# Latent attention: heads made in groups of four, half of them inside the attention, with the modulation sums moved behind them

## The chip, the cores and the metric

The kernel runs on one core of a Trainium2 chip. The metric is the device time of one execution in microseconds (us). A matmul runs on PE and its weights are loaded by PEld; DVE, ACT and POOL are the vector, scalar and GpSimd engines; SP issues most of the DMAs. Every engine works through its own list of instructions in order, and waits there for what it needs from another engine.

## The reference

Two layers of an encoder over 1024 tokens of width 1024. The change lies in the first layer's mixer, a latent attention with 16 heads. Cut to that:

```python
proj = h @ w_in                                   # 1024 x (384 + 256 + 32)
q = (rms_norm(q_lat, g_qa) @ w_qb).reshape(B, S, 16, 96)
kv = (rms_norm(kv_lat, g_kva) @ w_kvb).reshape(B, S, 16, 64 + 64)
q = concat(q[..., :64], rope(q[..., 64:]))
k = concat(kv[..., :64], k_rope of all heads)
v = kv[..., 64:]
q, k = rms_norm(q, g_q), rms_norm(k, g_k)
o = softmax(q k^T * 96 ** -0.5) v                 # all 1024 keys for each of 1024 queries
return o.reshape(B, S, 1024) @ w_o
```

`rms_norm(x) = x * rsqrt(mean(x * x) + eps) * g`. Around the mixer stand a norm with a shift, scale and gate that come from a conditioning vector: `mod = silu(c) @ ada_w + ada_b`, six vectors of 1024 for each layer. An MLP follows, and then a second layer with a dilated attention and an MLP.

## The kernel before

Every large product is made from fp16 high and low parts in three matmuls: `mm3` multiplies high by high (L532), high by low (L533) and low by high (L534). The program in order of time: the norm, the input projection and the latents (`latT`, transposed, in fp16 parts); the **heads stage**, 119 to 265 us; the **attention**, to 613 us; then the output projection, the MLP and the second layer.

**The heads stage** (`mla`, the loop `for hf in range(2)`) has two passes over the 8 tiles of 128 tokens. Pass 0 makes heads 0 to 7, pass 1 heads 8 to 15. A tile is two groups of four heads: for each group PE makes the queries `pq` (9 matmuls of 384 columns) and the keys and values `pkv` (6 of 512 columns), each into one of the 8 PSUM banks. From the banks ACT squares them; DVE sums the squares (`hms`; L954 is a small TENSOR_SCALAR that adds the rope part of the key, `krss`); `rstd` (L126) turns sums into factors, with Ln and Exp on ACT (L132, L133) and three small DVE steps (L134 to L136); DVE scales the bank's contents into `st`; POOL turns the rope columns (`rope_q`, four operations, L635 to L638) and multiplies the rope part of the key by the factor (L973); ACT rounds `st` to fp16 (L981); POOL takes the low part from that (L982), and SP stores the tile `s` to a DRAM buffer `qkv`. A tile's banks come free when DVE has scaled them.

Inside pass 0 stand the last two quarters of the latents and the weights of pass 1 (`heads_load`, `heads_split`; L156 and L161 are the two steps of a split). Inside pass 1 stand the first loads of the attention, since heads 0 to 7 are whole by then: `fetch(h)` reads `q` and `k` of a head from `qkv` with transposing DMAs (L842), `ones(h)` loads a row of ones and the values, and `rowmax(0)` makes the 16 partial row maxima of head 0: one matmul of 512 columns into a bank `pmx` (L893) and one TENSOR_REDUCE on DVE (L895), each. `topmost`, `turn` and `mrow` turn the maxima into a row of `q`, which the scores of that head need.

**The attention** (L1181) is written out by hand as 128 slots, one for each of 16 heads and 8 tiles of 128 keys, and `pin_from` keeps every engine to the written order. In a slot n PE makes the scores (`scores`, 6 matmuls of 512 columns, L1207 to L1209, into two banks `pss`), two row maxima of a head to come, and the product with the values of slot n-3 (`av`, 24 small matmuls); POOL takes the low part of the weights of slot n-1 (L1226, `pp`); ACT makes the weights of slot n (`weights`: two Exp that read `pss`, L1218, and one rounding, L1219). DVE takes the maxima, and ends a head (`finish`). The PSUM banks are three of kind "s" (scores), three of kind "t" (row maxima and everything else) and two of kind "av". In every fourth slot `ada_step` adds one row block of the modulation matrices to a sum (`ada_sum`, L270 for the first, L271 for the others: DVE, 128x1024, from SBUF to SBUF); after eight of them PE and DVE finish the vector (`ada_end`).

Of the kernel before, what the change touches and what calls it, by code (L numbers as in the profile page):

```python
# [9 lines left out]
F32 = mybir.dt.float32  # L10
F32R = mybir.dt.float32r
F16 = mybir.dt.float16
# [3 lines left out]
ALU = mybir.AluOpType  # L16
# [25 lines left out]
class K:  # L42
# [83 lines left out]
    def rstd(self, ms, n, name, up=False, y=None):  # L126

        nc = self.nc
        y = self.sm(name + "y", n) if y is None else y
        l = self.sm(name + "l", n)  # L130
        t = self.sm(name + "t", n)
        nc.scalar.activation(l, ms, AF.Ln, bias=self.eps_y if up else self.eps)  # L132
        nc.scalar.activation(y, l, AF.Exp, scale=-0.5)  # L133
        nc.vector.scalar_tensor_tensor(t, ms, EPS * 2.0 ** 26 if up else EPS, y, op0=ALU.add, op1=ALU.mult)  # L134
        nc.vector.scalar_tensor_tensor(t, t, -0.5, y, op0=ALU.mult, op1=ALU.mult)
        nc.vector.scalar_tensor_tensor(y, t, 1.5, y, op0=ALU.add, op1=ALU.mult)  # L136
        return y
# [517 lines left out]
    def mla(self, xs, ada0, xs1, mods, tail):  # L655
# [5 lines left out]
        lt = lambda k, c, t: LT[t // 4][k][c // 2][:, c % 2, (t % 4) * P : (t % 4 + 1) * P]  # L661
        krw = self.M("krw", [P, 8, 32])
# [22 lines left out]
        with tc.tile_pool(name="psA", bufs=2, space=PSUM, reuse_waits="tile") as psp:  # L685
# [38 lines left out]
            def latents(tp, lats, m, pt):  # L724
# [7 lines left out]
                if tp % 2 == 0:  # L732
                    for k, x in enumerate(self.pair(self.G, "latT", (P, 2, 512))):
                        LT[half][k].append(x)
# [109 lines left out]
        def ones(h):  # L844

            hd = heads[h]
            nc.sync.dma_start(out=hd["kh"][QK : QK + 1, :], in_=self.onerow)
            v = hd["v"] = self.G("hv", (P, 8, 129), F16)
            nc.gpsimd.memset(v[:, :, 128:129], 1.0)
            nc.sync.dma_start(out=v[:, :, 0:128], in_=qkv[h][:, 384:512].rearrange("(t p) e -> p t e", p=P))  # L850
# [73 lines left out]
        with tc.tile_pool(name="psB", bufs=8, space=PSUM, reuse_waits="tile") as psp:  # L924
            B = lambda name: psp.tile([P, 512], F32, tag="b", name=self.nm(name))
            raw = None
            for hf in range(2):
                w = hw[hf]
                for t in range(NT):
# [12 lines left out]
                    st = [self.G("st", (P, 4, 192 if half else 256), F32) for b in range(2)]  # L942
                    s16 = [self.G("s16", (P, 4, 512), F16) for b in range(2)] if half else None
# [12 lines left out]
                    if half:  # L956
                        for b in range(2):
                            self.parts(s16[b][:, :, 448:512], s16[b][:, :, 384:448], kv4[b][:, :, 64:128], 2.0 ** -7)
                    i = (hf * NT + t) * 16
                    r = self.rstd(ms, 16, "hr", half, rall[:, i : i + 16] if half else None)  # L960
                    for b in range(2):
                        if not half:
                            nc.scalar.activation(st[b][:, :, 192:256], kv4[b][:, :, 64:128], AF.Copy)
# [3 lines left out]
                        if half:  # L967
                            nc.vector.scalar_tensor_tensor(st[b][:, :, 96:160], kv4[b][:, :, 0:64], 64.0,
                                                           rk.broadcast_to([P, 4, 64]), op0=ALU.mult, op1=ALU.mult)
                        else:  # L970
                            nc.vector.tensor_tensor(st[b][:, :, 96:160], kv4[b][:, :, 0:64],
                                                    rk.broadcast_to([P, 4, 64]), op=ALU.mult)
                        nc.gpsimd.tensor_tensor(st[b][:, :, 160:192], rk.broadcast_to([P, 4, 32]),  # L973
                                                kr[:, t : t + 1, :].broadcast_to([P, 4, 32]), op=ALU.mult)
                    for b in range(2):
                        h0 = hf * 8 + b * 4
                        if half:
                            self.rope_q(st[b][:, :, 64:96], t)
                            nc.vector.tensor_tensor(st[b][:, :, 0:64], st[b][:, :, 0:64],
                                                    gt[:, 0:64].unsqueeze(1).broadcast_to([P, 4, 64]), op=ALU.mult)  # L980
                            nc.scalar.activation(s16[b][:, :, 0:192], st[b], AF.Copy)  # L981
                            nc.gpsimd.tensor_tensor(s16[b][:, :, 192:384], st[b], s16[b][:, :, 0:192], op=ALU.subtract)  # L982
                            nc.sync.dma_start(out=qkv[h0 : h0 + 4, ts, :].rearrange("h t e -> t h e"), in_=s16[b])
                            continue
# [12 lines left out]
                    elif half:  # L997
                        for f, x in {0: ((fetch, 0),), 1: ((ones, 0), (fetch, 1)), 2: ((ones, 1),), 5: ((fetch, 2),),
                                     6: ((ones, 2),)}.get(t, ()):
                            f(x)  # L1000
                        for j in {3: (0, 1, 2), 4: (3, 4, 5), 5: (6, 7)}.get(t, ()):
                            [rowmax(0, j, b, B("pmx")) for b in range(2)]
                        if t == 5:
                            topmost(0)
                        elif t == 6:
                            turn(0, B("pmt"))
                            mrow(0)
# [14 lines left out]
        if half:  # L1022
            self.nseen += 1
            s_ = self.seen[:, self.nseen - 1 : self.nseen]
            for _ in range(2):
                nc.gpsimd.tensor_tensor(rall, rall, rall, op=ALU.mult)
            nc.vector.tensor_reduce(s_, rall, op=ALU.add, axis=AX.X)
# [1814 lines left out]
```

## Time and profile before

| | us |
|---|---|
| median of 3 runs | 3013.63 (3011.02 to 3015.2) |
| the profiled execution | 3010.92 |
| its span in the trace | 3009.1 |
| heads stage, first matmul of pass 0 to first score | 119.3 to 265.4 |
| attention, first score to the last product | 265.4 to about 613 |
| attention, 111 slots from 283 to 578 us | 2.66 each |

The profile gives busy time for each engine as a whole, for each stretch of time and for each group of like instructions ("line engine op out<-in xcount | busy, mean ns of one | idle time before, by what ended it"). An instruction's row in the timeline reads: start, duration, engine, line, operation, out<-in, and in brackets the idle time before it with what ended that. "PE pmx <- DVE mx" is a wait of PE for a bank `pmx` that DVE still read.

### The profile page before, as it was taken

The numbers are of one execution on the slowest core, as the hardware profiler recorded it, in microseconds if no ns is written. First come the engines' busy times: TensorE is split into PE (matmuls) and PEld (weight loads), VectorE is DVE, ScalarE is ACT, GpSimd is POOL, SyncE is SP. The second block draws the span as 40 slices with busy tenths as digits, with TensorE's granted clock in tenths as the row PEclk, the third lists the DMA queues.
The fourth block names the chain that finished last, engine by engine and source line by source line (L and its number), as shares of the span: only waits on it lengthen the run. The fifth ranks groups of instructions, "written<-read, shape, count | busy, mean of one in ns | idle before, by whom it ended". The sixth has DMA issues, their size and how long they took to land. (4 is left out here: it accounts for less than half of the span.)

```text
span 3009.1 us, 54541 instructions
## 1 busy us (share of the span) xinstructions
PE 2830.6 (94%) x20148; PEld 1678.5 (56%) x20148; DVE 2272.5 (76%) x4991; ACT 1660.7 (55%) x3411; POOL 938.6 (31%) x1372
## 2 busy tenths in 40 slices
PE   6877999999999999999999989998997989999998
PEld 5634566644444444443468878877885444444443
DVE  6687777648988876689758877776886789779565
ACT  4645888825455533542227877776664355555331
POOL 6688888800111000001123434353552002110010
PEclk9988999999999999999999999999999999999999
DMA  6264555424755689555536656665666556457663
GB/s 208 73 175 127 114 103 107 137 78 134 258 193 188 236 246 314 184 192 191 210 114 140 156 130 157 154 134 123 140 143 165 146 187 217 154 180 257 231 197 91
DMA packets 556656, 503.07 MB, mean 167 GB/s; under 512 B 275638, under 2 KB 448995, under 8 KB 556379
## 3 DMA queue, kind: packets, MB, share of 16 engines
q1 hardware_dynamic: 520698, 400.74, 47.4%
q0 software_dynamic: 25248, 87.22, 7.8%
q10 hardware_dynamic: 10432, 11.54, 1.5%
q8 instruction: 159, 2.61, 0.4%
q14 instruction: 119, 0.97, 0.1%
HBM read 317.40 MB, written 125.12 MB: 147 GB/s over the span
## 5 line engine op out<-in xcount | busy, mean ns | idle before, releaser
L532 PE MATMUL psm<-hf,wf 128*128 128x512 f16 x896 | 341.1, 381 | 5.0 <-ACT wf L156 5.0
L534 PE MATMUL psm<-hf,wf 128*128 128x512 f16 x896 | 335.7, 381 | 10.5 <-DVE wf L161 10.5
L533 PE MATMUL psm<-d,d 128*128 128x512 f16 x896 | 340.5, 380 | 4.7 <-DVE d L161 4.7
L533 PE MATMUL psm<-hf,wf 128*128 128x512 f16 x896 | 340.8, 380 | 0.0
L534 PE MATMUL psm<-d,d 128*128 128x512 f16 x896 | 340.4, 380 | 0.0
L532 PE MATMUL psm<-d,d 128*128 128x512 f16 x896 | 334.6, 379 | 0.3 <-ACT d L156 0.3
L1226 POOL TENSOR_TENSOR pp<-p,pp 128x1024 f16<-128x1024 f32 x125 | 275.4, 2209 | 56.3 <-ACT pp L1219 38.8
L532 PE MATMUL psproj<-wqk,hTp 128*128 128x256 f16 x1024 | 283.6, 277 | 0.0
L533 PE MATMUL psproj<-wqk,hTp 128*128 128x256 f16 x1024 | 282.9, 276 | 0.0
L534 PE MATMUL psproj<-wqk,hTp 128*128 128x256 f16 x1024 | 282.6, 276 | 0.0
L156 ACT ACTIVATE d<-ufr 128x1024 f16<-128x1024 f32 x112 | 117.8, 1052 | 207.9 <-PE psm L534 170.4
L895 DVE TENSOR_REDUCE mx<-pmx 128x1 f32<-128x512 f32 x256 | 172.9, 687 | 78.9 <-PE pmx L893 77.6
L161 DVE SCALAR_TENSOR_TENSOR d<-ufr,d 128x1024 f16<-128x1024 f32 x112 | 136.3, 1217 | 75.0 <-ACT d L156 74.9
L1218 ACT ACTIVATE p<-pss 128x512 f32<-128x512 f32 x256 | 149.9, 590 | 40.9 <-PE pss L1209 39.3
L2321 ACT ACTIVATE pd<-pd,dnb 128x192 f32<-128x192 f32 (+2 forms) x384 | 167.2, 436 | 4.3 <-POOL y L2250 2.2
L534 PEld LDWEIGHTS <-wf 128*128 128x128 f16 x896 | 87.8, 98 | 122.5 <-DVE wf L161 18.1
L532 PEld LDWEIGHTS <-wf 128*128 128x128 f16 x896 | 87.8, 98 | 113.2 <-ACT wf L156 10.8
L534 PEld LDWEIGHTS <-d 128*128 128x128 f16 x896 | 87.7, 98 | 110.5 <-issue 5.6
L271 DVE SCALAR_TENSOR_TENSOR adacc<-adaw,cond,adacc 128x1024 f32<-128x1024 f32 (+1 forms) x98 | 129.0, 1316 | 25.5 <-DMA adaw<-in_ada_w 24.6
L532 PEld LDWEIGHTS <-d 128*128 128x128 f16 x896 | 87.9, 98 | 106.3 <-issue 2.0
L533 PEld LDWEIGHTS <-d 128*128 128x128 f16 x896 | 87.7, 98 | 106.0 <-issue 1.6
L533 PEld LDWEIGHTS <-wf 128*128 128x128 f16 x896 | 87.9, 98 | 104.9 <-issue 1.8
(434 smaller groups left out, 8132.1 us busy)
## 6 DMA issues: line engine op xcount, KB each, us to landing
ufr<-uf SPq DMA_DIRECT2D x112, 512.0 KB
w2r<-in_mlp_w SPq DMA_DIRECT2D x96, 512.0 KB
adaw<-in_ada_w SPq DMA_DIRECT2D x80, 512.0 KB
w1r<-in_mlp_w SPq DMA_DIRECT2D x64, 512.0 KB
wqkr<-in_dil_w_in SPq DMA_DIRECT2D x96, 256.0 KB
wvr<-in_dil_w_in SPq DMA_DIRECT2D x34, 512.0 KB
qkv<-s SPq DMA_DIRECT2D x32, 512.0 KB
uf<-ub POOLq DMA_DIRECT2D x32, 512.0 KB, 3.8
```

The lines of the kernel that those rows point to most:

```text
L156: nc.scalar.activation(hi, src, AF.Copy, scale=scale)
L161: return nc.vector.scalar_tensor_tensor(lo, src, scale, hi, op0=ALU.mult, op1=ALU.subtract, accum_out=self.seen[:, self.nseen - 1 : self.n ...
L271: return self.nc.vector.scalar_tensor_tensor(acc, w, c, acc, op0=ALU.mult, op1=ALU.add)
L532: mm(out, lh, rh, start=first, stop=False)
L533: mm(out, lh, rl, start=False, stop=False)
L534: mm(out, ll, rh, start=False, stop=last)
L895: nc.vector.tensor_reduce(maxes[h][:, 2 * j + b : 2 * j + b + 1], ps, op=ALU.max, axis=AX.X)
L1218: nc.scalar.activation(p[:, b * 512 : (b + 1) * 512], ps[b], AF.Exp, scale=1.0 / self.ss)
L1226: eng.tensor_tensor(q[:, 1], p, q[:, 0], op=ALU.subtract)
L2321: nc.scalar.activation(p[:, e, lo:hi], p[:, e, lo:hi], AF.Exp, scale=1.0 / self.ss, bias=nb[:, e : e + 1], accum_out=stat[:, g, t, 1, 2 * ...
```

## The change

The heads stage now makes only heads 0 to 7, group by group: `group_pair` takes one group of four heads and two token tiles, so 2 groups of 4 pairs, in place of 16 tiles of 8 heads. The matmuls and the steps behind them are the same ones; a pair fills 4 banks. The latents and the weights of heads 8 to 15 stay in it, at the first five pairs. At the second group's first pair `fetch(0)` is issued, behind its third pair all 16 row maxima of head 0 and `fetch(1)`, behind its last `turn`, `mrow` and the values of head 0.

Heads 8 to 15 are two groups of 8 tiles, so 16 **items** (`group_item`). They go into the attention: item i begins in slot 2 + (23 i + 2)//5, so an item in every four or five slots, the last in slot 71, and each is spread over seven slots: queries' matmuls, sums, scales and keys' matmuls, sums, scales, rounding, low part and store. `pq` and `pkv` of an item are banks of kind "t", where a bank is held from the matmuls to the scaling two slots later. An item's squares, Ln, Exp and rounding go to ACT at the ends of slots, its three `rstd` steps for queries and again for keys, now 4 elements wide in place of 16, to DVE, and rope, key part and low part to POOL between the attention's own low parts. `ones` is cut into the row of ones and `values`; loads of a head come two slots later than before.

`ada_step` is called in every eighth slot up to slot 76 and then in every third, in place of every fourth throughout, so that its last step falls in slot 132, behind the last scores. The check sum over all factors (`norms`) moves from ahead of the attention to slot 136.

The diff, cut to its core:

```diff
-            for hf in range(2):
+            for g, p in [(g, p) for g in range(2) for p in range(4)] if half else ():
+                self.group_pair(g, p, B, lt, hw[0], kr, krss, rall, gt, qkv)
...
+                if g == 1:
+                    if p == 0:
+                        fetch(0)
+                    elif p == 2:
+                        ones(0)
+                        for j in range(8):
+                            [rowmax(0, j, b, B("pmx")) for b in range(2)]
+                        topmost(0)
+                        fetch(1)
+                    elif p == 3:
+                        turn(0, B("pmt"))
+                        mrow(0)
+                        values(0)
+            for hf in range(0 if half else 2):
...
+    def group_item(self, n, lt, w, kr, krss, rall, gt, qkv):
...
+        return ([(0, "mm", q_mm), (1, "late", q_sum), (2, "late", q_mul), (2, "mm", k_mm), (3, "late", k_sum), (4, "late", k_mul)]
+                + [(0, "end", q_sq), (1, "end", q_ln), (2, "end", k_sq), (2, "end", turned), (3, "end", k_ln), (4, "end", k_rope),
+                   (5, "end", high), (6, "end", low)])
...
+            for i in range(16):
+                for o, where, f in item(i):
+                    n = 2 + (23 * i + 2) // 5 + o
+                    if where == "mm":
+                        put(n, f, PT, to=late)
+                    else:
+                        put(n, f, to={"late": late, "end": end}[where])
...
+            put(N + 8, norms, to=end)
...
-                if h > 2:
-                    put(8 * h - 18, fetch, h)
-                    put(8 * h - 14, ones, h)
+                if h > 1:
+                    put(8 * h - 16, fetch, h)
+                    put(8 * h - 13, ones, h)
+                put(8 * h - 6, values, h)
...
-                if n % 4 == 1:
+                if n % 8 == 1 if n < 76 else n % 3 == 0:
                     self.ada_step(psp, "t", 2)
```

The step of an item that ends its key sums reads:

```python
        def k_sum():
            c["mk"] = ms = self.sm("mk", 4)
            nc.vector.tensor_reduce(ms, e4(c.pop("sk"), 64), op=ALU.add, axis=AX.X)
            nc.vector.tensor_scalar(ms, ms, krss[:, t : t + 1], 1.0 / QK, op0=ALU.add, op1=ALU.mult)
            self.nseen += 1
            nc.vector.scalar_tensor_tensor(c["s16"][:, :, 384:448], kv4()[:, :, 64:128], 2.0 ** -7, c["s16"][:, :, 448:512],
                                           op0=ALU.mult, op1=ALU.subtract, accum_out=self.seen[:, self.nseen - 1 : self.nseen])
```

How that moves instructions is seen on two engines. On DVE, in slots 5 to 7 of the attention before (`mx` are row maxima, `adacc` a modulation sum, `ll` and `O` the end of head 0):

```order
L895 TENSOR_REDUCE mx_2979<-pmx_3213 128x1
L895 TENSOR_REDUCE mx_2979<-pmx_3231 128x1
L270 TENSOR_SCALAR adacc_3254<-adaw_2891,cond 128x1024
L895 TENSOR_REDUCE mx_2979<-pmx_3265 128x1
L895 TENSOR_REDUCE mx_2979<-pmx_3283 128x1
L1254 RECIPROCAL ll_3299<-pav_2933 128x4
L1255 TENSOR_TENSOR O_3298<-pav_2933,ll_3299 128x4x64
```

The same engine after the change, in slots 4 and 5, with the steps of item 0 behind the maxima (`gqt` and `rall` are the factor, `st` the scaled queries, `mk` the key sums, `s_454` the fp16 tile):

```order
L909 TENSOR_REDUCE mx_2317<-pmx_2316 128x1
L909 TENSOR_REDUCE mx_2317<-pmx_2335 128x1
L141 SCALAR_TENSOR_TENSOR gqt_2350<-mq_2298,rall 128x4
L142 SCALAR_TENSOR_TENSOR gqt_2350<-gqt_2350,rall 128x4
L143 SCALAR_TENSOR_TENSOR rall<-gqt_2350,rall 128x4
L1196 TENSOR_TENSOR st_2354<-pq_2233,rall 128x4x96
L1197 TENSOR_TENSOR st_2354<-st_2354,gt 128x4x64
L909 TENSOR_REDUCE mx_2317<-pmx_2387 128x1
L909 TENSOR_REDUCE mx_2317<-pmx_2405 128x1
L1291 TENSOR_REDUCE mk_2420<-sqk_2372 128x4
L1292 TENSOR_SCALAR mk_2420<-mk_2420,krss 128x4
L1294 SCALAR_TENSOR_TENSOR s_454_2373,seen_165<-pkv_2357,s_454_2373 128x4x64
```

A maximum that frees a bank of kind "t" stood behind another maximum, or now and then behind a modulation sum; now five or three operations of an item stand between two slots' maxima.

On POOL, the low parts of the attention's weights before:

```order
L1226 TENSOR_TENSOR pp_3160<-p_3159,pp_3160 128x1024
L1226 TENSOR_TENSOR pp_3204<-p_3203,pp_3204 128x1024
L849 MEMSET hv_3257 128x8
L1226 TENSOR_TENSOR pp_3248<-p_3247,pp_3248 128x1024
L1226 TENSOR_TENSOR pp_3306<-p_3305,pp_3306 128x1024
```

And after, with the rope of item 0 (`rqu`, `rqw`), its key part (L1206) and its low part (L1212) between them:

```order
L1369 TENSOR_TENSOR pp_2304<-p_2303,pp_2304 128x1024
L642 TENSOR_TENSOR rqu_2376<-st_2354,cg 128x128
L643 TENSOR_TENSOR rqw_2377<-st_2354,sg 128x4x16
L644 TENSOR_TENSOR rqw_2377<-st_2354,sg 128x4x16
L645 TENSOR_TENSOR st_2354<-rqu_2376,rqw_2377 128x4x32
L1369 TENSOR_TENSOR pp_2368<-p_2367,pp_2368 128x1024
L1369 TENSOR_TENSOR pp_2430<-p_2429,pp_2430 128x1024
L1206 TENSOR_TENSOR st_2354<-rall,kr 128x4x32
L1369 TENSOR_TENSOR pp_2482<-p_2481,pp_2482 128x1024
L1369 TENSOR_TENSOR pp_2537<-p_2536,pp_2537 128x1024
L1212 TENSOR_TENSOR s_454_2373<-st_2354,s_454_2373 128x4x192
```

Six operations of an item now stand among the low parts of five slots, on an engine that had one operation a slot.

More of the change, by code (lines that the diff above doesn't have):

```diff
@@ L1022, in mla @@
         if half:
[L1023 to L1027, printed above, removed]
[L1028 to L1029 removed]
+            item = lambda i: self.group_item(i, lt, hw[1], kr, krss, rall, gt, qkv)
+            return self.attention(heads, fetch, ones, values, rowmax, topmost, turn, mrow, tail, item, rall), None
         O = [[[None] * 4 for _ in range(2)] for _ in range(2)]
@@ L1184, in attention @@
+    def attention(self, heads, fetch, ones, values, rowmax, topmost, turn, mrow, tail, item, rall):
         nc, tc = self.nc, self.tc
```

190 lines of the change are left out of this document (141 added, 49 removed).

## The prediction

> **What bounds the kernel now.** I read the busy time by stretches first, then the groups of instructions, then the waits, and single rows last. The profiled execution took 3010.92 us, 2.7 below the median of the runs, and its span is:
>
> ```profile
> span 3009.1 us, 54541 instructions
> ```
>
> The busy time by stretches, for the heads stage as a whole, nine dense us of it, its second pass, the first six slots of the attention, and 111 later slots. Behind the two times stands the length, then each engine's busy time with its instructions, the granted TensorE clock, and DMA:
>
> ```profile
> core 0: us, PE busy (x) PEld busy (x) DVE busy (x) ACT busy (x) POOL busy (x), PEclk, DMA share, GB/s
> 119.30:265.40 146.10, 104.54 (x511) 51.65 (x509) 123.44 (x292) 73.73 (x184) 111.79 (x193) 0.88 0.52 146
> 173.00:182.00 9.00, 9.00 (x49) 4.69 (x48) 8.28 (x20) 5.62 (x15) 8.68 (x14) 1.00 0.34 117
> 195.00:265.40 70.40, 42.40 (x197) 19.97 (x197) 56.22 (x131) 28.76 (x71) 53.80 (x91) 0.83 0.67 174
> 265.40:283.00 17.60, 16.23 (x97) 7.14 (x98) 13.00 (x25) 11.63 (x17) 15.59 (x16) 0.72 0.34 110
> 283.00:578.00 295.00, 288.35 (x3651) 178.90 (x3647) 213.06 (x333) 248.89 (x359) 245.63 (x125) 1.00 0.50 106
> ```
>
> The two stages have different limits. In the second pass PE works 42.40 of 70.40 us, while DVE is busy 56.22: about 28 us of PE lie idle there. In the attention PE works 288.35 of 295.00 us and bounds it, but the others are not idle: a slot of 2.66 us (295.00/111) holds 1.92 us of DVE, 2.24 of ACT and 2.21 of POOL. Who holds PE up there, from the first score on (us in total, times, longest):
>
> ```profile
> PE pss L1207 <- DVE st L968: 11.7, 1, 11.7
> PE pmx L893 <- DVE mx L895: 8.0, 7, 1.3
> ```
>
> The first wait is the end of the heads stage. The second comes seven times, behind a modulation sum that stood ahead of a row maximum. The sums' durations (shortest, median, longest in ns) and the groups of the 111 slots on POOL and DVE:
>
> ```profile
> L271 DVE SCALAR_TENSOR_TENSOR adacc<-adaw,cond,adacc x98: 739/1276/3189, 12.5 to 2784.4; 128x1024 f32<-128x1024 f32 x70, 128x512 f32<-128x512 f32 x28
> ```
>
> ```profile
> L1226 POOL TENSOR_TENSOR pp<-p,pp 128x1024 f16<-128x1024 f32 x112 | 247.5, 2214 | 49.5 <-ACT pp L1219 35.4 <-PE pmx L893 13.4 <-POOL pp L1226 0.4
> ```
>
> ```profile
> L895 DVE TENSOR_REDUCE mx<-pmx 128x1 f32<-128x512 f32 x223 | 152.1, 688 | 77.3 <-PE pmx L893 76.0
> L271 DVE SCALAR_TENSOR_TENSOR adacc<-adaw,cond,adacc 128x1024 f32<-128x1024 f32 x21 | 38.5, 1831 | 0.0
> ```
>
> A sum takes 1.28 us in the middle case and up to 3.19; 1.83 is the mean in the attention, where POOL is busy 83% (245.63/295.00) with operations of 2.21. So DVE waits there for POOL: 0.55 us for an operation of this kind on average (1.83 less 1.28), 1.9 at most.
>
> **The start of the attention: -56.** The second pass goes: 70.40 us. What comes back is the tail. The change asks for head 0 behind the fifth of eight pairs; a pair is as much work as a tile of the first pass. Single rows: the fifth tile's last low part on POOL; one of the second pass's transposed loads on SP, the last of head 0; the first row maximum on PE; and the first matmul of the last tile:
>
> ```profile
> 175.65 1.64 POOL L982 TENSOR_TENSOR s<-st,s 128x768 f16<-128x768 f32 x1
> ```
>
> ```profile
> 206.40 2.04 SPq L842 DMA_TRANSPOSE k<-qkv  x1
> ```
>
> ```profile
> 215.36 0.38 PE L893 MATMUL pmx<-k,q 96*128 96x512 f16 x1 [1.10 <-ACT s L156]
> ```
>
> ```profile
> 248.09 0.34 PE L532 MATMUL pq<-wh,latT 128*128 128x384 f16 x1
> ```
>
> The store can leave at 177.3 (175.65 + 1.64). In the trace the first maximum runs 9.0 us behind the issue of head 0's last load (215.36 - 206.40), and then waits for ACT, so 9.0 is an upper bound: the maxima begin at 186 or somewhat later. All 16 stand ahead of the last pair's matmuls on PE. They cost DVE 11 us (16 of 0.69) among the third pair's steps, some 12.5 in all, so I let the last pair begin at 194 to 195. The last tile of before takes 17.3 us from first matmul to first score (265.40 - 248.09). A pair has as many matmuls and the same steps behind them, but nothing of another head between; I take 14.5, from 13 to 17. So the first score falls at about 209, with 202 to 215 as bounds: -56, from -63 to -50. `turn` and `mrow` of head 0, now behind the last pair, are covered by those 14.5 us, and would add what they exceed them by.
>
> **PE's work that moves: +44.** Heads 8 to 15 come back into a stage that PE bounds. The pace of matmuls of 384 and of 512 columns (consecutive starts), and a slot from score to score:
>
> ```profile
> 250.70 0.33 PE L533 MATMUL pq<-wh,latT 128*128 128x384 f16 x1
> 250.86 0.33 PE L534 MATMUL pq<-wh,latT 128*128 128x384 f16 x1
> ```
>
> ```profile
> 421.04 0.38 PE L1207 MATMUL pss<-q,k 97*128 97x512 f16 x1
> 421.26 0.38 PE L1208 MATMUL pss<-q,k 96*128 96x512 f16 x1
> ...
> 423.51 0.38 PE L1207 MATMUL pss<-q,k 97*128 97x512 f16 x1
> ```
>
> One item is 9 x 0.163 + 6 x 0.217 = 2.77 us (0.163 and 0.217 are means over such rows, 0.16 and 0.22 here); 16 items are 44. A free slot is 2.47 us long.
>
> **What the items do to the other engines: +25.** This decides the sign. An item comes every 4.6 slots. PE needs 4.6 x 2.47 + 2.77 = 14.1 us, or 14.7 if all that the 111 slots held is counted (288.35/111 = 2.60 a slot, the ends of heads and of modulation vectors with it); I take 14.4. ACT needs 4.6 x 2.24, and not over 3.6 for the item (28.76 for 8 tiles of two groups): 13.9 at most. POOL needs 4.6 x 2.21 and 53.80/16 = 3.4: 13.6. DVE's groups in the heads stage, tile by tile of two groups:
>
> ```profile
> L964 DVE TENSOR_TENSOR st<-pq,rall 128x384 f32<-128x384 f32 x32 | 17.7, 552 | 0.9
> L979 DVE TENSOR_TENSOR st<-st,gt 128x256 f32<-128x256 f32 x30 | 17.1, 582 | 0.0
> L952 DVE TENSOR_REDUCE hms<-sq 128x8 f32<-128x768 f32 x16 | 15.1, 943 | 8.3 <-ACT sq L948 8.1
> L968 DVE SCALAR_TENSOR_TENSOR st<-pkv,rall 128x256 f32<-128x256 f32 x32 | 13.2, 413 | 0.0
> L161 DVE SCALAR_TENSOR_TENSOR s<-pkv,s 128x256 f16<-128x256 f32 x32 | 12.9, 411 | 1.5 <-ACT s L156 1.5
> L954 DVE TENSOR_SCALAR hms<-hms,krss 128x8 f32<-128x8 f32 x16 | 11.5, 722 | 0.0
> L953 DVE TENSOR_REDUCE hms<-sqk 128x8 f32<-128x512 f32 x16 | 10.8, 673 | 0.0
> L895 DVE TENSOR_REDUCE mx<-pmx 128x1 f32<-128x512 f32 x16 | 10.2, 678 | 0.0
> L134 DVE SCALAR_TENSOR_TENSOR hrt<-hms,rall 128x16 f32<-128x16 f32 x16 | 7.8, 488 | 6.4 <-ACT rall L133 6.3
> ...
> L135 DVE SCALAR_TENSOR_TENSOR hrt<-hrt,rall 128x16 f32<-128x16 f32 x16 | 5.8, 363 | 0.5
> L136 DVE SCALAR_TENSOR_TENSOR rall<-hrt,rall 128x16 f32<-128x16 f32 x16 | 3.0, 185 | 0.4
> ```
>
> Per item: scales 0.55 + 0.58 + 0.41, the value part 0.41, half of each sum 0.47 + 0.34, the small TENSOR_SCALAR 0.72, and the three `rstd` steps 1.04, twice, since queries and keys now have their own: 5.6 us. Part of that is waiting already. The small TENSOR_SCALAR's shortest, median and longest:
>
> ```profile
> L954 DVE TENSOR_SCALAR hms<-hms,krss x16: 220/273/1659, 127.7 to 259.6; 128x8 f32<-128x8 f32 x16
> ```
>
> Its longest, 1659 ns, is a POOL low part's length (1.64). Against a shortest of 0.22 the mean holds 0.50 of waiting; if a step of 16 elements takes 0.17 undisturbed, as L136's mean of 0.185 suggests, two sets of `rstd` hold 1.0, and the second scale (0.58, against 0.41 for as many elements in L968) 0.2. So 1.7 of the 5.6 is waiting, and 3.9 work. In the attention POOL's operations are longer; at the 0.55 us of the modulation sums, and about five meetings an item (two in the queries' factor and scale, one in the TENSOR_SCALAR, two in the keys' factor), the waiting is 2.75: 6.65 per item. The sums themselves come half as often while items run: 38.5/111 = 0.35 a slot, so -0.8 for 4.6 slots. DVE then needs 4.6 x 1.92 - 0.8 + 6.65 = 14.7 us, more than PE's 14.4, and takes its work from three engines in a fixed order. The densest stretch of the heads stage, where it does these same steps, has it busy 8.28 of 9.00 us, 92%. At 92% an item's time is 16.0: 1.6 us of stall, 16 times, +25. The route of the stall: `pq` and `pkv` take one of the three "t" banks, two stay for the maxima, and a maximum behind five small operations frees its bank late; an item's Ln on ACT waits for DVE's sums too, and behind it stand the Exp that free the score banks.
>
> The Trainium skill, page "SBUF — State Buffer", section "Who interferes with whom", says that DVE and GpSimd share a port pair that is locked for a whole instruction, and that a DVE operation with two SBUF inputs, or one such as tensor_scalar in its two-port mode, blocks behind a GpSimd instruction that reads SBUF. The trace agrees: 0.22 to 1.66 us for one TENSOR_SCALAR of eight elements, 1.28 to 3.19 for a modulation sum.
>
> **The rest: -2.** Four of the seven stalls at a modulation sum, 8.0/7 = 1.1 us each, lie in slots that lose their sum: -4. The last vector, finished in slot 132, stands in the tail behind the last scores: eight small matmuls and their DVE step, +2. Loads that come two slots later (`fetch` 16 slots ahead) have slots of 2.5 us to land, against the 9.0 above: nothing, unless head 8 or 12 comes late; head 12's load is issued in slot 80, three slots behind the last item's store. `norms` leaves the head of the attention, where the wait was for L968, and costs nothing behind it.
>
> **The sum.** -56 + 44 + 25 - 4 + 2 = +11: 3010.9 + 11 = 3022 for the profiled execution, and 3024 or 3025 for a median that lies 2.7 higher; I say 3024. Without any stall of the items it would be -14.
>
> **The rivals.** *The small steps fit into gaps* (faster). DVE in the 111 slots is idle 82 of 295 us, and a mean of 1.83 between 1.28 and 3.19 would be reached if only 6 of the 21 sums met POOL at full length (21 x 0.55/1.91). If the items' steps mostly miss POOL too, DVE needs 8.0 + 3.9, near 12 of 14.4 us, and the stall is a short one, 0.3 per item, 5 in all: -56 + 44 + 5 - 2 = -9, and 3005 by the median. Against it: five operations in a row meet a POOL that is busy 13.6 of 14.4 us. *The port is met at random* (much slower). Each meeting then costs half of POOL's 2.21 us times its 83%, 0.9 us; five are 4.5 on top of 3.9 of work, DVE needs 8.0 + 8.4 = 16.4, at 92% 17.8, a stall of 3.4 per item, 54 in all: -56 + 44 + 54 - 2 = +40, 3054. It decides against the gain from a stall of 0.9 us per item (14/16) on. For it: POOL runs its low parts almost without a break. Against it: 0.55 was seen, not 0.9. The page named above gives this time if every one of the five steps arrives while POOL holds the port. *The change does not do what it says*, or a head's load comes late: a load late by a whole slot or two at head 8 or 12 is 2.5 to 5 us each beside the forecast.
>
> **How the numbers follow.** The forecast has 0.47, the small stall 0.36, the random port 0.15, the rest 0.02. About 0.2%, 6 us, is what a measurement of this kernel can tell from no change. Of the forecast's 0.47, by the bounds of the start (7 us each way) and DVE's share, 0.33 lies above +6, 0.12 within 6, 0.02 below. Of the small stall's 0.36, 0.27 lies below -6 and 0.09 within. With the random port and the rest, that makes faster 0.29, same 0.21, slower 0.50. The range: no stall and an early start is -14 to -18, so 2998 at the low end; the high end leaves the upper half of the random port out, 3046. The forecast's own range is 3012 to 3034.
>
> **What would show it.** Right, if the first score comes near 209; if slots with items average 16.0/4.6, near 3.5 us, against 14.4/4.6 = 3.1 without stalls; if PE waits about 25 us for maxima or score banks until slot 77; if the 4-element `rstd` steps and the TENSOR_SCALAR show lengths up to 2 us. Wrong, if DVE is busy under 85% in those slots with short steps (the first rival), or if PE waits mostly for something else: a load of a head, ACT's rounding, or a weight tile that POOL made late.

## The result and the profile after

The change makes the kernel slower: 3036.78 us by the median of four runs, against 3013.76 (four runs of the kernel before, one more than above); the ratio is 1.0078 (95% interval 1.0061 to 1.0096), 18 to 29 us. The forecast was 3024, slower, with a range of 2998 to 3046: the direction came out, and about half of the size. The profiled execution has a span of 3035.3 us, some 26 more than before.

Where that comes from is read off at four places: first score, score of slot 78 (behind the last item), last product with the values, first matmul of the output projection. Before they stand at 265.4, 477.4, 611.0 and 612.6 us, now at 204.5, 490.3, 627.4 and 632.9. The start is won by 61 us, slots 0 to 77 take 74 more, the slots behind them 3, the step to the projection 4. That is +20, and the rest of the program, which no line of the diff touches, adds 6 in these two executions (its own section is below).

Busy time in slots 0 to 77, before:

```profile
265.40:477.40 212.00, 206.19 (x2495) 124.56 (x2496) 153.61 (x242) 176.49 (x254) 178.67 (x99) 0.98 0.50 107
```

The same slots after (length, then PE, PEld, DVE, ACT, POOL, granted clock, DMA):

```profile
204.50:490.30 285.80, 258.09 (x2715) 149.22 (x2716) 224.04 (x452) 216.75 (x381) 229.70 (x189) 0.96 0.43 96
```

PE waits 27.7 us in this stretch where it waited 5.8, and its granted clock is lower. DVE, which the prediction made the bound, is busy 224.04 of 285.80, 78%. What PE waited for there, in us, times and longest:

```profile
PE pq L539 <- DVE mx L909: 7.1, 5, 3.1
PE pav L1384 <- DVE O L1398: 7.0, 5, 2.2
PE pmx L907 <- DVE mx L909: 5.2, 5, 1.6
PE pss L1350 <- DVE st L1201: 4.7, 1, 4.7
PE psot L1409 <- DVE st L1196: 3.3, 2, 1.7
PE pkv L539 <- DVE mx L909: 1.7, 3, 0.9
```

The wait for `st` is the end of the heads stage, ahead of the first score. The others are few and long: five waits for a maximum's bank ahead of an item's queries hold 7.1 us, five for the end of a head 7.0. So the stalls do not come item by item, as DVE falling behind would make them. They come where one long step on DVE stands ahead of what PE needs next. The items' small steps on DVE over these slots:

```profile
L1292 DVE TENSOR_SCALAR mk<-mk,krss 128x4 f32<-128x4 f32 x16 | 19.6, 1228 | 0.6
L278 DVE SCALAR_TENSOR_TENSOR adacc<-adaw,cond,adacc 128x1024 f32<-128x1024 f32 x7 | 14.1, 2021 | 0.0
L142 DVE SCALAR_TENSOR_TENSOR gqt<-gqt,rall 128x4 f32<-128x4 f32 x16 | 9.5, 596 | 0.6
L141 DVE SCALAR_TENSOR_TENSOR gqt<-mq,rall 128x4 f32<-128x4 f32 x16 | 7.4, 460 | 0.0
L141 DVE SCALAR_TENSOR_TENSOR gkt<-mk,rall 128x4 f32<-128x4 f32 x16 | 5.6, 349 | 0.0
L143 DVE SCALAR_TENSOR_TENSOR rall<-gqt,rall 128x4 f32<-128x4 f32 x16 | 2.6, 162 | 0.5
```

A step of four elements that meets nothing takes 0.16 us (L143). The TENSOR_SCALAR takes 1.23 on average. Its shortest, median and longest:

```profile
L1292 DVE TENSOR_SCALAR mk<-mk,krss x16: 229/1108/1955, 225.7 to 480.3; 128x4 f32<-128x4 f32 x16
```

Against the shortest, 0.23, 16 of its 19.6 us are waiting, and with L141 and L142 it is 31, 1.9 us per item. Fourteen of the sixteen end 0.02 to 0.03 us behind the end of an operation on POOL; the two of 0.23 us were issued as a low part ended. That POOL is what they wait for is read from such rows; no run moves POOL's work away.

One of the worst slots, number 43, in single rows. DVE:

```profile
360.31 0.40 DVE L1291 TENSOR_REDUCE mk<-sqk 128x4 f32<-128x256 f32 x1
360.75 1.58 DVE L1292 TENSOR_SCALAR mk<-mk,krss 128x4 f32<-128x4 f32 x1
...
363.34 0.42 DVE L1398 TENSOR_TENSOR O<-pav,ll 128x256 f32<-128x256 f32 x1
```

POOL, ACT and PE at the same time:

```profile
360.18 4.21 POOL L1369 TENSOR_TENSOR pp<-p,pp 128x1024 f16<-128x1024 f32 x2
```

```profile
362.36 0.30 ACT L134 ACTIVATE gkl<-mk,misc 128x4 f32<-128x4 f32 x1 [2.04 <-DVE mk L1292]
```

```profile
363.27 0.23 PE L1384 MATMUL pav<-hv,pp 128*128 128x65 f16 x1 [2.19 <-DVE O L1398]
```

POOL takes two low parts in a row. DVE's step of four elements starts during the first, and is done when that ends. Behind it on DVE stand the steps that end head 4, which free the banks of the product with the values, and PE waits 2.19 us for them. ACT waits 2.04 for the same step with its Ln, and the Exp of the slot stands behind that.

### The profile page after: what moved, and what is told of

It reads as the page before. It is cut to its first block, busy times and chain, and to the rows that moved or that the text cites. A ratio compares the mean times of both kernels' runs of the same rounds, so it can differ in the third digit from the quotient of the medians.

```text
span 3035.3 us, 54748 instructions
## 1 busy us (share of the span) xinstructions
PE 2850.4 (94%) x20148; PEld 1686.1 (56%) x20148; DVE 2309.9 (76%) x5095; ACT 1671.6 (55%) x3459; POOL 948.0 (31%) x1372
```

## The experiments

Two theories of the stalls, *Meeting* and *Bank*, were set against the one of the prediction. *Load*, the prediction's: DVE has more to do in an item's time than fits, so the stall follows its sum. *Meeting*: DVE has time, but single port waits, above all that of the TENSOR_SCALAR ahead of ACT's Ln (a port wait is a DVE step that lasts until an operation on POOL ends), hold PE where it stands close behind. *Bank*: two "t" banks are too few for the maxima. Times below are ratios to the kernel before on the same chip, with their 95% interval. "PE idle" is the sum of the idle time before PE's matmuls in slots 0 to 77: 5.8 us before, 27.7 after. Slots and idle time are those of the one profiled execution of each kernel.

| run | ratio | slots 0 to 77, us | PE idle there |
|---|---|---|---|
| before | 1 | 211.9 | 5.8 |
| after | 1.0078 (1.0061 to 1.0096) | 285.8 | 27.7 |
| all heads first | 0.9984 (0.9975 to 0.9994) | 209.9 | 4.6 |
| no scalar step | 1.0018 (1.0007 to 1.0029) | 268.2 | 18.3 |
| no small steps | 0.9966 (0.9953 to 0.9979) | 258.8 | 8.2 |
| sums after items | 1.0049 (1.0031 to 1.0068) | 270.3 | 18.8 |
| four slots, clear of ends | 1.0103 (1.0086 to 1.0119) | 283.8 | 30.9 |
| four slots, on the ends | 1.0149 (1.0132 to 1.0166) | 294.9 | 31.3 |
| before, new sums | 1.0001 (0.9992 to 1.0011) | 203.2 | 1.4 |
| before, two banks | 1.0067 (1.0050 to 1.0084) | 225.7 | 12.6 |
| four slots, no scalar step | 1.0016 (1.0006 to 1.0026) | 268.7 | 15.6 |
| four slots, no small steps | 0.9987 (0.9978 to 0.9997) | 251.4 | 4.0 |
| no small steps, sums moved | 0.9988 (0.9977 to 1.0000) | 252.4 | 5.0 |
| four slots, no small steps, sums as before | 0.9948 (0.9934 to 0.9963) | 257.6 | 5.9 |

**All heads first.** Sixteen pairs ahead of the attention, no items, the first loads and maxima spread over the third and fourth groups, the sums as before.

```diff
-            for g, p in [(g, p) for g in range(2) for p in range(4)] if half else ():
-                self.group_pair(g, p, B, lt, hw[0], kr, krss, rall, gt, qkv)
+            for g, p in [(g, p) for g in range(4) for p in range(4)] if half else ():
+                self.group_pair(g, p, B, lt, hw[g // 2], kr, krss, rall, gt, qkv)
...
-            for i in range(16):
+            for i in range(0):
```

> All 16 heads in groups of four ahead of the attention, no item inside it, modulation sums in every fourth slot as before the change; only the form of the heads stage is new. If the loss comes from the items inside the attention (both the theory of the prediction, too much DVE work, and the later one, single long port waits), this is about the kernel before: 3014, from 3008 to 3020. If the group form itself costs (more steps that wait, later loads), it is above 3020, and part of the 23 us of the change is not the items' doing.

0.9984: not slower than before, first score at 265.3 and projection at 613.0, both as before. The new form of the heads stage costs nothing; the loss is made inside the attention.

**No scalar step.** The TENSOR_SCALAR of the items' keys is folded into ACT's Ln (scale and bias) and into the first step behind it; what is computed is the same.

```diff
-            nc.vector.tensor_scalar(ms, ms, krss[:, t : t + 1], 1.0 / QK, op0=ALU.add, op1=ALU.mult)
...
-            c["k"] = self.rstd_open(c.pop("mk"), 4, "gk", True, rk)
+            l = self.sm("gkl", 4)
+            nc.scalar.activation(l, c["mk"], AF.Ln, bias=krss[0][:, t : t + 1], scale=1.0 / QK)
+            nc.scalar.activation(rk, l, AF.Exp, scale=-0.5)
...
+            stt(x, c.pop("mk"), krss[1][:, t : t + 1], rk, op0=ALU.add, op1=ALU.mult)
+            stt(x, x, -0.5 / QK, rk, op0=ALU.mult, op1=ALU.mult)
+            stt(rk, x, 1.5, rk, op0=ALU.add, op1=ALU.mult)
```

> The changed kernel, with the items' small TENSOR_SCALAR (keys' sums) folded into the scale and bias of ACT's Ln and into the first step behind it, so that ACT's Ln stands behind a reduction alone. Meeting theory: this step holds 16.0 of the 31 us that the items' small steps wait on DVE in the attention, and ACT waits behind it; about half of the 27.6 us of PE's idle time in slots 0 to 77 and of the 12 us of slow pace goes: 3018, from 3012 to 3025. Bank theory (two banks left for the row maxima are too few, whatever the steps wait): no change, 3034 or more.

1.0018: one instruction of four elements per item was worth 0.6% of the whole program, 18 us by the ratios. PE's idle time fell by 9.4 us and the slots by 17.6; the rest of that is pace (below). At the output projection 12.8 of it are left (620.1 against 632.9), since the heads stage ends 2.6 us later in this run and the stretch behind slot 77 takes 2.3 more. The bank theory, which expected no change, falls as a whole account.

**No small steps.** As well, the three refining steps of an item's two factors are left out.

```diff
-            self.rstd_end(*c.pop("q"))
+            c.pop("q")
```

> As the one before, and without the three refining steps of the items' factors on DVE (left out, so the factors are those of Ln and Exp alone): the items have no step left that reads two operands from SBUF except the gain's multiplication. Meeting theory: PE's idle time in slots 0 to 77 falls from 27.6 us to under 8, what is left being the modulation sums, and the pace loss with it: 3005, from 3000 to 3012, so the kernel before is beaten. Bank theory: the banks are as scarce as ever, 3025 or more. Load theory of the prediction: an item's DVE work falls from 6.0 to 3.6 us, no stall left either, so it does not differ from the meeting theory here.

0.9966, faster than before. PE's waits in slots 0 to 77:

```profile
PE pq L539 <- DVE mx L913: 5.0, 3, 2.4
PE pss L1355 <- DVE st L1205: 4.7, 1, 4.7
PE psot L1414 <- DVE mx L913: 1.6, 4, 0.4
```

The waits behind a head's end are gone; of the 5.0 us, two waits of 2.4 stand behind a modulation sum of 3.27 in slots 34 and 66. The items keep their bank, their matmuls and their large steps, so the bank alone does not make the loss. Load and meeting agree here.

**Sums after items.** All modulation sums of the attention in every second slot from 76 on.

```diff
-                if n % 8 == 1 if n < 76 else n % 3 == 0:
+                if n >= 76 and n % 2 == 0:
```

> The changed kernel, with all modulation sums of the attention behind the items: every second slot from 76 on, last one again in slot 132. If the sums are what makes the items' stalls long (the two worst slots, 34 and 66, have a sum of 2.92 us behind the keys' step), idle time in slots 0 to 77 falls by 8 to 10 and the pace loss by 4, and the denser sums behind give back up to 7: 3026 to 3032. If the sums only happen to be near, 3034 to 3042.

1.0049: 15.5 us off slots 0 to 77, and 9.8 given back behind them, where the attention now takes 146.9 us in place of 137.1. The sums share in the stalls, but are not all of them: 18.8 us of idle time stay without any sum.

**Four slots.** An item in every fourth slot, at two phases against the ends of heads (slots 10, 18, 26 and so on), with the sums behind the items.

```diff
-                    n = 2 + (23 * i + 2) // 5 + o
+                    n = 1 + 4 * i + o
```

> The changed kernel with an item in every fourth slot from slot 1 on, which gives each item the same place against the ends of heads: the keys' small steps never fall into a slot that ends a head. The sums stand behind the items, as in the run with the sums moved. Load theory: in 4 slots PE needs 12.7 us and DVE 13.0, more over than before, so stalls grow to 1.5 us an item or more: 3040 or slower. Meeting theory: the item's port waits stay, but meet nothing else; PE idle in the items' slots falls from 27.6 to about 15: 3018, from 3010 to 3027.

1.0103, slower than the change (3047.8), where the meeting theory had expected 3018: that number was wrong, and load's, 3040 or slower, came out. What speaks against load comes with the next two runs. Why meeting's number was wrong is seen in the TENSOR_SCALAR itself (shortest, median, longest), and in the waits:

```profile
L1292 DVE TENSOR_SCALAR mk<-mk,krss x16: 967/1914/1957, 223.9 to 454.6; 128x4 f32<-128x4 f32 x16
```

```profile
PE pq L539 <- DVE mx L909: 13.3, 11, 1.7
PE pmx L907 <- DVE mx L909: 8.6, 7, 1.6
```

In the change the median was 1.1 us. With a fixed rhythm nearly every item's step starts 0.2 to 0.3 us behind the start of a low part on POOL, and lasts until that ends: 1.9 us for fifteen of the sixteen, and in fourteen slots PE stands 1.6 to 1.7. So a wait of that length stops PE even with nothing else in the slot. The queries' steps L141 or L142 last 1.56 in fifteen slots of the same run, and in none of these does PE stop: there no Ln and Exp stand behind, which is the likely reason and was not tried by itself.

With n = 3 + 4i, the other phase:

> The same with the items two slots later, from slot 3 on: the same work in the same density, but the keys' small TENSOR_SCALAR of every second item falls into a slot that ends a head, ahead of the steps that free the banks of the head's product, as in slots 10, 42 and 74 of the changed kernel (1.7, 2.2 and 2.2 us of PE idle there). Load theory: the same as from slot 1 on, within 4 us. Meeting theory: eight such slots at 2 us and their slow pace, 15 to 25 us slower than from slot 1 on.

1.0149, 13 us slower by the medians (3060.8 against 3047.8) at the same work and density; load had expected no difference over 4 us, meeting 15 to 25. The waits that came in:

```profile
PE pav L1384 <- DVE O L1398: 20.8, 8, 2.6
```

Eight waits for the end of a head, 2.6 us each, as expected of the eight slots in which the step falls on one. But others went (those ahead of the queries fell from 13.3 to 6.4, those ahead of the maxima from 8.6 to 0.2), and PE's idle time in sum is the same, 31.3 against 30.9. What is longer is PE's work, 263.65 us in place of 252.94, at a lower granted clock. Slots 0 to 77, clear of the ends, then on them:

```profile
204.40:488.20 283.80, 252.94 (x2714) 147.67 (x2715) 229.78 (x444) 216.85 (x382) 226.22 (x190) 0.99 0.39 84
206.10:501.10 295.00, 263.65 (x2715) 152.54 (x2716) 221.37 (x444) 216.58 (x382) 226.62 (x191) 0.93 0.37 81
```

So the phase costs, as meeting said, but here through the length of the single stalls, which the clock answers (last section), and not through their sum.

**Four slots, no scalar step.** The first phase, with the step folded away, and the sums in the slots of the change.

> Items in every fourth slot from slot 1 on, as in the slowest pair of runs, with the small TENSOR_SCALAR folded into ACT's Ln and the first step behind it, and the modulation sums in the slots of the changed kernel. With the step in place each item held PE for 1.6 to 1.7 us behind one wait of 1.9. If it is that step's place ahead of ACT's Ln (waits of 1.56 on the queries' steps stopped nothing there), PE's idle time in slots 0 to 77 falls from 30.9 to under 12, and the time to 3012, from 3006 to 3020. If the density alone makes the stall (load theory), the wait moves to the next step and idle time stays above 20: 3028 or more.

1.0016, 26 us below the same rhythm with the step by the ratios, though the sums are back among the items; the time, 3022.7, lies between the two that were expected. In PE's idle time 15.6 us stay, not under 12, behind seven ends of heads and a few maxima. DVE in this run:

```profile
204.60:473.30 268.70, 253.12 (x2715) 146.62 (x2716) 233.22 (x436) 218.50 (x382) 233.15 (x191) 0.99 0.48 104
```

It is busy 87% (233.22 of 268.70), more than after the change (78%), with little over half of the idle time. Load's account fails here: how much of the time DVE is busy does not set the stall.

**Four slots, no small steps** (the refining steps left out again):

> The same, and without the three refining steps of the items' factors on DVE (left out). Four slots hold 12.7 us of PE and 4 x 1.92 + 3.6 = 11.3 of DVE, so there is no reason left to wait but the sums: idle time in slots 0 to 77 about 5, 3004, from 2999 to 3010. If the bank alone costs, 3015 or more.

0.9987: idle time 4.0 us, and the projection begins 12.5 us earlier than before, the gain that was expected of the whole program. The total shows only 4 of them and lies at 3011.9, just outside what was expected; where the rest went is the last section's matter.

**No small steps, sums moved** (items in the slots of the change, refining steps left out).

```diff
-                if n % 8 == 1 if n < 76 else n % 3 == 0:
+                if (n == 1 or n % 8 == 7) if n < 76 else n % 3 == 0:
```

> Items in the slots of the change, without the scalar step and the refining steps (left out), and the modulation sums below slot 76 in slots 1, 7, 15, 23 and so on in place of 1, 9, 17 and so on. With the sums in their old slots 34 and 66 held PE for 2.4 us each behind a sum of 3.27, and lost 1 to 1.5 more to slow pace. If a sum costs only where it stands between the keys' sums and the maxima, idle time in slots 0 to 77 falls from 8.2 to about 4, 6 us faster than with the old slots, 3002. If any slot is as bad, no change, 3008.

The stalls of slots 34 and 66 are gone, idle time is 5.0 where it was 8.2, and the last product with the values comes 6.4 us earlier, as expected. Of that the projection keeps 4.1 (599.5 against 603.6): the last vector's sixteen small matmuls just ahead of it take 3.41 us at half clock here, and 1.84 in the run above without small steps. The whole program does not show it: 0.9988 against 0.9966, and 3011.7 is slower than either expectation.

**Before, new sums.** The kernel before with the new slots of the sums alone.

> The kernel before with nothing but the new slots of the modulation sums (every eighth, from 76 on every third). By the prediction four of seven stalls of 1.1 go and the last vector in the tail costs 2: -2, 3012. If the last vector costs more, since its matmuls stand ahead of the output projection on PE (the changed kernel has 3.2 us there between two sets of transposes), 3014 to 3018.

No difference (1.0001). Its parts are both there: the attention ends 6.1 us sooner from first score to last product (4.3 of it PE's idle time, 1.9 the last vector's matmuls, which stood in it), and the step from there to the projection takes 6.2 us where it took 1.6. PE's rows there after the change show why:

```profile
628.50 0.66 PE L1409 MATMUL psot<-ident,O 128*128 128x128 f32 x4 [0.89 <-DVE O L1398]
629.00 3.16 PE L357 MATMUL psac<-ones,adacc 128*128 128x1 f32 x16
632.02 1.09 PE L1409 MATMUL psot<-ident,O 128*128 128x128 f32 x4
```

The last vector's small matmuls hold PE for 3 us between the two last sets of transposes; at full clock they take 1.9.

**Before, two banks.** The kernel before with two "t" banks, one bank unused.

```diff
-            PT = lambda name: psp.tile([P, 512], F32, tag="t", bufs=3, name=self.nm(name))
+            PT = lambda name: psp.tile([P, 512], F32, tag="t", bufs=2, name=self.nm(name))
```

> The kernel before with two banks in place of three for row maxima and transposes, one bank unused: what an item's bank takes from the attention, without any item. If two banks are enough as long as DVE is free, the slots of 2.47 us stay and only those with a sum or a transpose grow: 3014 to 3022. If two banks make the maxima wait in every slot, 0.2 us or more each, 3040 or slower, and a good part of the change's loss is the bank.

1.0067, 20 us, between the two cases. The waits:

```profile
PE pmx L893 <- DVE mx L895: 9.7, 7, 1.8
PE psot L1266 <- DVE mx L895: 2.9, 8, 0.4
```

Of the 13.8 us that slots 0 to 77 are longer, half is idle time. Slots of 2.47 to 2.49 us stay as they were; a sum that waits for POOL now costs 1.75 in place of 1.25, transposes 0.3 to 0.4, and the first three slots 3.4 more. So the bank does matter where something long stands on DVE, and is free where nothing does, which the runs without small steps show with the items in place.

**Four slots, no small steps, sums as before** (refining steps left out):

> Items in every fourth slot from slot 1 on without scalar step and without the refining steps (left out), and the modulation sums in every fourth slot throughout, as in the kernel before, so that the last vector's matmuls stand in slot 113 and not between the last transposes and the output projection. The tail term: 4 us come off between the last product with the values and the output projection (5 to 6 us there with the new slots, 1.6 in the kernel before). If the items' slots take the eight more sums without a stall, 4 us faster than with the new slots, 0.3 to 0.4% faster than before, 3003. If every second sum stalls PE by 1.1, as in the kernel before, nothing is gained: 3010.

0.9948 (0.9934 to 0.9963), 11 to 20 us faster than before, the fastest of all. The projection follows the last product by 1.6 us again. Slots 0 to 77:

```profile
206.60:464.20 257.60, 251.66 (x2735) 147.70 (x2736) 208.31 (x350) 218.49 (x382) 236.95 (x192) 0.99 0.55 125
```

```profile
PE pmx L911 <- DVE mx L913: 2.4, 4, 0.6
PE pq L539 <- DVE mx L913: 1.6, 4, 0.4
```

DVE is busy 81% and POOL 92%, both more than after the change, and PE waits 5.9 us, as in the kernel before.

## Why the prediction was right, and which of its steps were not

**Start, -56.** Measured -61: first score at 204.5, inside the bounds of 202 to 215, nearer the early one. The first row maximum ran at 179.6 and not at 186, the last pair began at 192.3, where 194 to 195 was taken, and from there to the first score it took 12.2 us, not 14.5.

**PE's work, +44.** Slots with an item's queries or keys and no wait last 3.93 to 3.95 or 3.76 to 3.77 us where a free one lasts 2.47: 1.47 and 1.30, the 2.77 of the working.

**Items on DVE, +25.** Here size and sign came out, but the step as the prediction put it, "At 92% an item's time is 16.0: 1.6 us of stall, 16 times", failed. DVE works 78% of these slots, under the 85% that the prediction itself named as a sign against it (though its steps are not short), and runs with 81 and 87% stall less. It needs 13.2 us in 4.6 slots (224.04/78 x 4.6), not 14.7, while 4.6 slots last 16.9. What holds is what stood below that: small steps wait for POOL's operations, 1.9 us an item where 2.75 was taken, and ACT's Ln and the maxima stand behind. The stall follows from where the wait falls. A TENSOR_SCALAR that lasts 1.9 us costs PE 1.6 to 1.7 at fourteen of sixteen items (four slots, clear of ends), one that falls on a head's end 2.6; the queries' waits cost almost nothing. Without the step, 13 of the 20 us at the projection are gone (18 of 23 by the ratios of the whole program). That the sum came out near (PE idle +22 us, with the sums' -4 in it) is luck, a coincidence of two prices, and no confirmation of the mechanism.

**A term that was missing: the pace.** A long stall is followed by slow matmuls. The row before the stall of slot 34, the first behind it and some later ones:

```profile
324.65 0.38 PE L907 MATMUL pmx<-k,q 96*128 96x512 f16 x1
328.51 0.32 PE L539 MATMUL pq<-wh,latT 128*128 128x384 f16 x1 [3.11 <-DVE mx L909]
...
330.05 0.53 PE L539 MATMUL pq<-wh,latT 128*128 128x384 f16 x1
330.37 0.53 PE L540 MATMUL pq<-wh,latT 128*128 128x384 f16 x1
```

Starts are 0.32 us apart where 384 columns take 0.163. The granted clock in the stall, behind it and after that (the column behind the five engines):

```profile
322.70:328.50 5.80, 2.70 (x40) 1.65 (x36) 5.76 (x8) 3.52 (x6) 4.08 (x3) 1.00 1.05 220
328.50:332.30 3.80, 3.79 (x13) 1.66 (x13) 2.41 (x9) 0.49 (x1) 2.48 (x2) 0.55 0.03 7
332.30:340.00 7.70, 6.06 (x71) 3.51 (x70) 5.97 (x11) 6.18 (x12) 3.90 (x3) 1.00 0.03 9
```

Over slots 0 to 77 the starts lose 18 us to slow pace after, 6 before (the excess of each start-to-start time over its usual one, idle time taken off): +12, which the prediction had not: half as much again as the idle time adds (22). Only a part is the granted clock, 0.96 over 285.80 us against 0.98 over 212.00: 11.4 less 4.2, some 7 us. The rest stands at full clock, for the most part in the start-to-start times that hold a stall.

**The rest, -2.** In the kernel with the new sums alone this is about as forecast up to the projection: idle time falls by 4.3 us, the last vector's matmuls leave the attention (1.9) and lengthen the step behind it by 4.6, so -1.5 from first score to projection. The 2 that was taken for the last vector is what its matmuls take at full clock; here they run at half. `norms` and the later loads cost nothing that shows.

**The sum, measured.** Up to the projection: -61 for the start; in slots 0 to 77 +44 for the items' matmuls, -4 for two vectors' matmuls that left these slots, +22 of idle time and +12 of pace; +3 behind slot 77 and +4 in the last step. That is +20 where +11 was forecast. The pace, at nothing in the forecast, is the largest term that was missed; the start, 5 us better than forecast, hides a part of it.

**The rivals.** That the small steps fit into gaps was wrong by its sum, but its time, 3005, is what the kernel without the small steps reaches. That the port is met at random (3054) was too much for the change. What it lacked is that the meeting need not be random: a fixed rhythm meets it every time. Its 0.9 us a meeting holds POOL's free 17%; if each of the five steps met POOL, it would be half of 2.21, 1.1 us, and the time above 3054. ACT's 3.6 us for an item is a tile's, twice an item's, which changes nothing, as ACT was not the bound.

The Trainium skill, page "SBUF — State Buffer", section "Who interferes with whom", says that issue order decides which of the two engines blocks. The four-slot runs agree: the same step, issued at another point of POOL's work, takes 1.9 us at the median there and 1.1 in the change.

## What to carry to other kernels

In this kernel, work that moved into a stage bounded by PE was paid for not by the sum of what it added to the other engines, but by its longest single waits and by what stood behind them in order, on its own engine and on the next one. One long stall of PE could cost more than two of half its length, since the clock fell behind it. So look first for a small operation that can wait long (here four elements behind a POOL operation of 2.1 us) with a release of PE's banks or another engine's step behind it, and take that one out; one folded TENSOR_SCALAR gave back 13 of the 20 us at the projection. An interleaving rhythm should be tried at more than one period and phase, since a fixed one can meet the wait every time.

## What the runs showed of the hardware that was not expected

**Half pace behind a short stall.** Stalls of 3.11, 3.10, 2.20, 2.19 and 1.67 us (slots 34, 66, 75, 43 and 11 after the change) were each followed by matmuls at about half pace; behind the first this lasts 3.4 us, 328.9 to 332.3. Stalls of 1.60 to 1.69 (slots 29, 36, 61 and 68) were not, and in the four-slot run thirteen of fourteen stalls of 1.6 to 1.7 us were not. The Trainium skill, page "TensorE: Matmul & The Clock Gate", section "HAM oscillation — how this bites in real kernels", names idle gaps above some 3.4 us; shorter ones suffice here.

The traces show what else decides it. In them the granted clock changes only at points that lie a multiple of 3.41 us apart, and a step of 3.41 us in which PE idled for about half of it or more is followed by one at half clock. The step that holds slot 11's stall (PE is busy 1.74 of 3.41 us) and the one behind it:

```profile
240.15:243.56 3.41, 1.74 (x15) 0.70 (x13) 3.31 (x9) 1.91 (x5) 3.41 (x4) 1.00 0.37 82
243.56:246.97 3.41, 3.41 (x31) 2.13 (x28) 2.46 (x8) 1.45 (x2) 2.13 (x3) 0.50 0.00 0
```

With four slots, on the ends, the stall of slot 27 is longer, 2.6 us, but falls across two steps. PE is busy 2.26 and 1.93 us in them, and the clock, the last column but two, stays:

```profile
306.65:310.07 3.42, 2.26 (x25) 1.05 (x21) 3.38 (x5) 1.47 (x2) 3.34 (x6) 1.00 0.52 170
310.07:313.48 3.41, 1.93 (x31) 1.41 (x32) 3.30 (x11) 2.53 (x5) 2.57 (x2) 1.00 0.28 64
313.48:316.89 3.41, 3.41 (x39) 2.10 (x38) 1.81 (x5) 2.10 (x4) 2.48 (x2) 1.00 0.02 5
```

Over slots 6 to 77 of the fourteen traces, all fifteen steps at full clock with 1.70 us or more of idle time were followed by one at half clock and none with 1.65 or less was; of the four in between, two were. Of the eight stalls of 2.6 us there, six fell so, of the fourteen of 1.6 to 1.7 one, which is where the 11 us between these two runs come from.

**A later stage that differs without an edit.** From the first matmul of the dilated projection to the last, the profile counts 753 us in the kernel before and in the one with all heads first, and 755 to 764 in the others, though no edit touches it. Part of it, some 5 us between the following two, is a transfer PE waits for, in the kernel before:

```profile
PE psav L2373 <- DMA pT<-ph: 21.8, 9, 6.2
```

And in the four-slot kernel without small steps:

```profile
PE psav L2542 <- DMA pT<-ph: 26.4, 11, 6.2
```

The granted clock of the stage is lower as well, 0.97 against 0.98. The stage is 11 us longer in that kernel, and so its 12.5 us at the projection became 4 at the end. What sets it is open. Differences of up to some 10 us between whole times of two kernels are therefore not put down to their edits alone here; the causes above are read up to the projection.
